# A split, modulated input kept in DRAM by the first of four passes and loaded by the other three

## The chip, the cores and the metric

One core of a Trainium2 chip. Its engines run side by side: PE (matrix products), DVE (vector), ACT (functions of one element, scaled copies), POOL, and SP, which here issues the DMAs. Each takes its instructions in the order that the build fixed, and waits at semaphores for the others. The metric is the device time of one execution in microseconds (us), lower is better.

## The reference

One layer for 4096 tokens of width 1024. `h = x * (1 + scale) + shift`, where shift, scale and gate come from a vector `c`; `proj = h @ w_in`, whose columns go to two kinds of heads; their outputs, normed and gated, are multiplied by `w_out`; then a layer norm.

```python
h = x * (1.0 + scale) + shift
proj = h @ w_in
# four heads of gated linear attention, in chunks of 64 tokens
S = d_n[..., None] * S + u_n                     # decay of the state, update
y_a = rms_norm(o_a, gla_norm_w) * silu(gla_og)
# four heads of the gated delta rule: convolution over 4 tokens, then per chunk
sol = triangular_solve(A + eye, rhs)             # unit lower triangular
v_new = u_n - w_n @ S
y_b = rms_norm(o_b, gdn_norm_w) * silu(gdn_og)
y = concatenate([y_a, y_b]) @ w_out
return layer_norm(ALPHA * x + (1.0 + gate) * y, ln_w, ln_b)
```

All of it is float32. The kernel takes operands of the large products in two parts of the type float32r: a head, which is the operand rounded, and a rest, which is what the head leaves. A product is three matmuls: head by head, head by rest, rest by head (`mm3`).

## The kernel before

The tokens are cut into 8 blocks of 512, the width into 8 k tiles of 128. Four passes go over all blocks, since the weights of one pass fill the room there is: two passes of gated linear attention with two heads each (GLA), then two of the delta rule with two heads each (GDN), then the output projection with the layer norm, block by block. What a pass makes of a block goes to DRAM (`y_spill`) until the end.

Every pass needs `h` of every block, in two parts. `prep_h` (L179 to L185) makes it anew each time: four loads `xt` of two k tiles each (512 KB), per k tile a modulation on DVE (L175), the head as a cast on ACT (L107), the rest as a subtraction on DVE (L64). The lines of `mod_split`:

```python
nc.vector.tensor_scalar(out=xt[:, j], in0=xt[:, j], scalar1=modc[:, 8 + k:9 + k],
                        scalar2=modc[:, k:k + 1], op0=mul, op1=add)
return split(xt[:, j], halves(hpool)(k))
```

`hpool` has 18 tiles of one part each: those of a block and one k tile more. `xpool` has three rooms of 512 KB; they serve `xt`, the raw weights of the next pass (`raw`) and some smaller things in turn.

The products of block n + 1 run while the recurrence and the norm of block n are worked off: `weave` lays a generator of small steps (`side`) into one of large products (`main`) and pins the order on PE by dependencies; where a small step stands among the products is written out by the numbers that the generators yield. The order on the other engines and on SP is a scheduler's. `h` of the next block is asked for right after a block's products.

In GLA a block's products are those for values (`pp<-wvl,h` in the first pass, `pp<-w,h` in the second), q, k and gate (`pp<-h,w`). Out of a low rank (`lr`, kept for the second pass in `lr_spill`) come the decays `e`, and from them W; the chunks' products are `pw<-VS,W`; `o` is scaled by its norm on DVE and transposed on PE (`pw<-ident,o`). The first block of all takes its products as the operands arrive (`first_block`).

In GDN a block has products for k, q, v and gate (all `pp<-h,w`), a convolution by three DVE steps each (`cacc`), the keys' sums of squares (`ssk`, on ACT by `jk`, then on DVE; `st` and `s` are the steps of its root), the products of keys (`AQ`) and the inverse of a triangular matrix. For the inverse the diagonal blocks of 32 go out (`u_spill`) and come back laid out for a solve on all partitions (`U`); the solve is a chain of 31 pairs of small DVE steps on `R`; `R` goes out (`r_spill`) and comes back as `Rd`, which DVE transposes to `Td` (L787). PE's products with `Td` and `Rd` put the inverse together, and the scan over chunks follows.

Of the kernel before, what the change touches and what calls it, by code (L numbers as in the profile page):

```python
# [13 lines left out]
F32 = mybir.dt.float32  # L14
F32R = mybir.dt.float32r
# [6 lines left out]
P = 128  # L22
D = 1024
KT = D // P  # 8 contraction tiles of the model width
TB = 512  # tokens of a block
# [6 lines left out]
def tile_hybrid(ctx, tc, xp, x, c, wada, bada, w_gla, w_vl, w_gdn, w_out, wup, bgate,  # L32
# [6 lines left out]

    ysp = nc.dram_tensor("y_spill", (NB, 4, P, 2, TB), F32).ap()  # L40
    lrsp = nc.dram_tensor("lr_spill", (NB, 80, TB), F32).ap()
# [6 lines left out]
    hpool = ctx.enter_context(tc.tile_pool(name="hpool", bufs=18))  # L48
# [3 lines left out]
    def share_banks(ph, n):  # L52
        """n of the 8 PSUM banks for the projections, the rest for everything else"""
        banks["proj"] = ph.enter_context(tc.tile_pool(name="pproj", bufs=n, space=PSUM))
        banks["work"] = ph.enter_context(tc.tile_pool(name="pwork", bufs=8 - n, space=PSUM))
# [15 lines left out]
    def keep_after(ins, other, reason):  # L71
        """the order of two instructions of an engine"""
# [4 lines left out]
    def in_order(ins):  # L77
        """functions that need a table keep their order on ScalarE, so that tables are loaded as
        seldom as the order has it"""
        if last_table[0] is not None:  # L80
            keep_after(ins, last_table[0], "table order")
        last_table[0] = ins
# [35 lines left out]
    # strict[c, j] = 1 where c > j  # L118
# [3 lines left out]
    # 1 + gate on every partition  # L122
# [11 lines left out]
    def mod_col(cb, wt, j, k):  # L134
        """column k of part j: 0 shift, 1 scale, 2 gate"""
# [27 lines left out]

    def halves(pool):
        return lambda k: [pool.tile([P, TB], F32R, name="h", tag="h") for _ in range(2)]
# [7 lines left out]
    def mod_split(xt, k):  # L173
# [3 lines left out]
        return split(xt[:, j], halves(hpool)(k))  # L177

    def prep_h(b):  # L179
        h = []  # L180
        for kk in range(4):
            xt = xpool.tile([P, 2, TB], F32, name="xt", tag="x")
            nc.sync.dma_start(out=xt, in_=xp[b, kk])
            h += [mod_split(xt, 2 * kk + j) for j in range(2)]
        return h  # L185

    def mm3(ps, lhs, rhs, first, last):
        """ps += lhs.T @ rhs, each (head, rest) of float32r: the three products that count."""
# [8 lines left out]
    def weave(side, main):  # L197
        """side's steps, each followed by as many of main's as it asks for; then the rest of main"""
# [13 lines left out]
    def rsqrt(pool, x, name):  # L212
        """x ** -0.5 of a small tile: a first guess from the exponent, and Newton's steps"""
# [13 lines left out]
    # a and b of the delta rule, by token  # L227
    abt = const.tile([P, NCH, 8], F32, name="abt")

    # ================= gate scalars of the delta rule =================  # L230
    # [token, head pair, (chunk, head of the pair)]
# [7 lines left out]
    def gate_scalars():  # L239
        tmp4 = xpool.tile([P, 8, P], F32, name="tmp4", tag="x")  # L240
        # mle[c, i] = 1 where c <= i
# [41 lines left out]
    # ================= gated linear attention, two heads a pass =================  # L283
    with ExitStack() as ph:
# [5 lines left out]
        # m64[64 * r + j, i] = 1 where j <= i  # L290
# [6 lines left out]
        # zero where a chunk of 64 starts  # L297
# [4 lines left out]
        # values of pass 0, and beside them the low rank gates and a and b: 256 + 16 + 8 columns  # L302
# [9 lines left out]
        # both parts of the gates' operands, one under the other: lr (head, head, rest), w (head, rest, head)  # L312
# [35 lines left out]
        def decays(t, lr):  # L348
            """exp of the sums of the log gates over a chunk of 64, in the four forms in use"""
# [26 lines left out]
        # W: left operand of [S' | o] = W.T [v ; S], rows (tokens, dk) of an even chunk,  # L376
        # (dk, tokens) of an odd one; columns (S', o) and (o, S')
# [17 lines left out]
        def from_k(kp, qt, W, e2, e4):  # L395
# [3 lines left out]
            # the two heads' operands lie in two halves of the array: a bank for each  # L399
# [19 lines left out]
        def values(t, b, wv, h, VS):  # L419
            """two token tiles at a time"""  # L420
# [32 lines left out]
        def finish(b, t, o, sg):  # L453
            """norm of o over a head, then its transpose times the norm's weight and the gate"""
# [20 lines left out]
        def weights():  # L475
            """v, q, k and gate of pass 1"""
# [6 lines left out]
        def first_block():  # L483
            """all products of a k tile as soon as its operands are there"""
            h, wt = [], {}
            ps = [proj_psum() for _ in range(3)] + [work_psum() for _ in range(8 - 3)]
            xt = None
            for k in range(KT):
# [16 lines left out]
                h.append(mod_split(xt, k))  # L505
# [23 lines left out]
        def block(t, b, h, W, VS, sg, first):  # L529
            """the block's products, and what follows each"""  # L530
            ahead = (t, b) == (1, NB - 1)  # weights of the next phase
# [30 lines left out]
        def before(st, VS):  # L562
            """chunks, norm and gate of the block before"""
# [9 lines left out]
        ws = []  # of the delta rule: columns of k, q, v, gate, two heads each  # L573
        for it in range(2 * NB + 1):
# [10 lines left out]
            if new:  # L585
# [5 lines left out]
                h = prep_h((it + 1) % NB)  # L591
# [5 lines left out]
    # ================= output projection and layer norm, by blocks =================  # L597
# [22 lines left out]
    def out_block(b, y, xres, lnw_sb, lnb_sb):  # L620
        for g in range(4):
# [6 lines left out]
            # the last tile of a block takes both halves at once, and so lets go of y as it goes  # L628
# [21 lines left out]
    # ================= gated delta rule, two heads a pass =================  # L650
    with ExitStack() as ph:
# [7 lines left out]
        # rows 0 to 63: the upper left inverses of 64; rows 64 to 127: products on the way  # L659
# [5 lines left out]
        def conv(t, b, i, ps):  # L665
            """causal convolution, i: 0 1 k, 2 3 q, 4 5 v; ps [128, 512]"""
# [14 lines left out]
        def decay_tiles(t, b, E):  # L681
            """E[j, (chunk, head), i] = exp(sum of g over j < c <= i), zero where j > i"""
# [20 lines left out]
        def sumsq(KQ, which, name):  # L703
            """sums of squares by token and RMS_EPS, and the transposes they were taken from"""
# [387 lines left out]
```

## Time and profile before

| | |
|---|---|
| median of 3 runs | 2206.84 us (2204.34 to 2214.05) |
| span of the profiled execution | 2214.4 us |
| PE busy | 2123.4 us (96%), 12868 matmuls |
| PE weight loads busy | 1789.0 us (81%), beside PE |
| DVE busy | 1593.8 us (72%) |
| ACT busy | 1078.2 us (49%) |
| DMA moved | 188.10 MB, mean 85 GB/s |

The page gives no time of the profiled execution beside its span; the span lies 0.3% above the median and as high as the slowest of the three runs. Busy time counts instructions at work, and matmuls overlap each other in their pipeline, so that a PE busy for 96% is not one at its peak. The clock in the rows is the share of full speed that PE was granted.

### The profile page before, as it was taken

What the parts mean: (1) busy time and instruction counts of PE and PEld (TensorE: products, weight loads), DVE (VectorE), ACT (ScalarE), POOL (GpSimd) and SP (SyncE); (2) the same over time, 40 slices, a digit from 0 to 9 for tenths busy, and PEclk for the clock granted to TensorE, in tenths of its full rate; (3) what the DMA queues carried; (4) which work ended last, traced back from release to release, by engine and by line L of the source; (5) the groups of instructions that cost most, each with busy time, mean ns of one, the idle gap of its engine ahead of it and who ended that gap; (6) DMA issues with size and microseconds to landing.
All of it is one profiled execution on the core that took longest, in us unless ns stands there. A gap on an engine that the chain in (4) does not pass through costs nothing.

```text
span 2214.4 us, 35705 instructions
## 1 busy us (share of the span) xinstructions
PE 2123.4 (96%) x12868; PEld 1789.0 (81%) x12868; DVE 1593.8 (72%) x4243; ACT 1078.2 (49%) x2685; POOL 205.4 (9%) x453
## 2 busy tenths in 40 slices
PE   6899999999999999999999999999999999999998
PEld 5788888878878778888888877888888777888886
DVE  7886776776577667867778677787677867766665
ACT  2655556645546545565554755556555462221110
POOL 1000000000000221011110121111111230000000
PEclk9999999999999989999999989999999999999999
DMA  7151123212113212121111321212112234353431
GB/s 279 65 164 51 54 89 98 74 66 87 52 51 128 79 34 64 52 65 46 37 63 63 103 72 34 64 52 65 48 36 62 61 93 148 143 198 135 140 107 76
DMA packets 89649, 188.10 MB, mean 85 GB/s; under 512 B 42704, under 2 KB 44800, under 8 KB 89472
## 3 DMA queue, kind: packets, MB, share of 16 engines
q1 hardware_dynamic: 89472, 185.82, 25.3%
q8 instruction: 101, 1.65, 0.3%
q14 instruction: 76, 0.62, 0.1%
HBM read 146.73 MB, written 39.06 MB: 84 GB/s over the span
## 4 chain that ended last, share of the span: by engine, by line
PE 66%; DVE 19%; ACT 4%; DMA 3%; issue 2%; SPq 0%; POOL 0%; DVEq 0%; ACTq 0%; POOLq 0%
PE pp L93 48%; PE pw L93 16%; PE pw L96 3%; DVE W L64 2%; DVE cacc L67 2%; DVE tp L64 2%; DVE R L64 2%; DVE e L64 1%; DMA xt<-xp 1%; DVE vp L64 1%; DVE xt L175 1%; ACT VS L107 1%; DVE o L64 1%; DVE h L64 1%; DVE bc L362 1%
## 5 line engine op out<-in xcount | busy, mean ns | idle before, releaser
L93 PE MATMUL pp<-h,w 128*128 128x512 f32 x4512 | 1147.3, 402 | 1.1 <-DVE W L64 1.1
L93 PEld LDWEIGHTS pp<-h,w 128*128 128x128 f32 x4512 | 828.3, 190 | 161.1 <-issue 1.7
L93 PE MATMUL pp<-w,h 128*128 128x512 f32 (+1 forms) x2112 | 421.1, 355 | 2.3 <-DVE w L64 1.1
L93 PEld LDWEIGHTS pp<-w,h 128*128 128x128 f32 x2112 | 349.4, 190 | 55.8 <-DVE w L64 1.7
L67 DVE SCALAR_TENSOR_TENSOR cacc<-u,convw_sb,cacc 128x512 f32<-128x512 f32 x288 | 220.7, 768 | 72.9 <-ACT cacc L99 70.1
L107 ACT CAST h<-xt 128x512 fp32r<-128x512 f32 x256 | 156.9, 619 | 133.4 <-PE pp L93 92.0
L64 DVE TENSOR_TENSOR h<-xt,h 128x512 fp32r<-128x512 f32 x256 | 175.1, 692 | 62.3 <-ACT h L107 38.4
L175 DVE TENSOR_SCALAR xt<-xt,modc 128x512 f32<-128x512 f32 x256 | 137.7, 554 | 28.3 <-DMA xt<-xp 27.8
L93 PE MATMUL pp<-wvl,h 128*128 128x280 f32 x744 | 117.1, 306 | 20.3 <-ACT h L107 19.1
L93 PEld LDWEIGHTS pp<-wvl,h 128*128 128x128 f32 x744 | 104.0, 196 | 23.6 <-ACT h L107 19.8
L99 ACT ACTIVATE rl<-mv,lnepscol 128x1 f32<-128x1 f32 x32 | 9.4, 295 | 225.3 <-DVE mv L641 211.3
L64 DVE TENSOR_TENSOR tp<-U,R 128x60 f32<-128x60 f32 (+24 forms) x496 | 115.4, 233 | 4.2
L64 DVE TENSOR_TENSOR R<-R,tp 128x60 f32<-128x60 f32 (+24 forms) x496 | 111.1, 224 | 4.6
L99 ACT ACTIVATE KQ<-cacc 128x512 f32<-128x512 f32 x64 | 40.5, 633 | 131.3 <-DVE cacc L67 131.1
L99 ACT ACTIVATE jk<-pw 128x128 f32<-128x128 f32 x256 | 71.8, 280 | 57.8 <-PE pw L96 52.6
L93 PE MATMUL pw<-VS,W 128*128 128x128 f32 x512 | 81.7, 283 | 4.1 <-DVE VS L443 2.8
L93 PE MATMUL pw<-S,KQ 128*128 128x128 f32 x512 | 85.0, 280 | 0.5 <-DVE S L67 0.5
L67 DVE SCALAR_TENSOR_TENSOR xres<-xres,pp 128x512 f32<-128x512 f32 x48 | 32.3, 682 | 71.9 <-PE pp L93 67.1
L107 ACT COPY u<-pp 128x512 f32<-128x512 f32 x96 | 56.4, 588 | 53.5 <-PE pp L93 45.9
L93 PEld LDWEIGHTS pw<-S,KQ 128*128 128x128 f32 x512 | 76.4, 195 | 6.3 <-DVE S L67 1.2
L107 ACT COPY o<-pw 64x256 f32<-64x256 f32 x128 | 46.8, 366 | 63.6 <-DVE VS L447 39.8
L99 ACT ACT_TABLE_LOAD x60 | 77.0, 1283 | 1.1
(328 smaller groups left out, 2926.3 us busy)
## 6 DMA issues: line engine op xcount, KB each, us to landing
xt<-xp SPq DMA_DIRECT2D x128, 512.0 KB
y_spill<-sg SPq DMA_DIRECT2D x32, 512.0 KB
yt<-y_spill SPq DMA_DIRECT2D x32, 512.0 KB
xres<-x SPq DMA_DIRECT2D x24, 512.0 KB
out_dram<-xres SPq DMA_DIRECT2D x24, 512.0 KB
mt<-wada SPq DMA_DIRECT2D x8, 1024.0 KB
raw<-w_gdn SPq DMA_DIRECT2D x16, 512.0 KB
U<-u_spill SPq DMA_DIRECT2D x64, 128.0 KB
```

The lines of the kernel that those rows point to most:

```text
L64: nc.vector.tensor_tensor(out=out, in0=a, in1=b, op=op)
L67: nc.vector.scalar_tensor_tensor(out=out, in0=a, scalar=s, in1=b, op0=op0, op1=op1)
L93: pe(nc.tensor.matmul(out, lhsT=lhsT, rhs=rhs, start=start, stop=stop))
L96: pe(nc.tensor.transpose(out, in_=in_, identity=identity))
L99: ins = nc.scalar.activation(out=out, in_=in_, func=func, **kw)
L107: nc.scalar.copy(out=out, in_=in_)
L175: nc.vector.tensor_scalar(out=xt[:, j], in0=xt[:, j], scalar1=modc[:, 8 + k:9 + k], scalar2=modc[:, k:k + 1], op0=mul, op1=add)
L362: nc.vector.tensor_tensor_scan(out=bc, data0=rmask, data1=mz, initial=0.0, op0=mul, op1=add)
```

## The change

In the first pass `make_h` does what `prep_h` did and then stores both parts of each k tile to a new DRAM tensor `h_spill` (`keep_h`: eight stores of 512 KB a block). In the other three passes `load_h` loads both parts of a k tile in one transfer of 512 KB, eight a block, straight into the operands, and there is no arithmetic on x. `hpool` now has 9 tiles of a pair each, the same room. The pools' other pairs follow (`halves`; `ypool` from 16 to 8). Comments are gone too.

```diff
+    hsp = nc.dram_tensor("h_spill", (NB, KT, P, 2, TB), F32).ap()
-    hpool = ctx.enter_context(tc.tile_pool(name="hpool", bufs=18))
+    hpool = ctx.enter_context(tc.tile_pool(name="hpool", bufs=9))
...
+    def pair(pool):
+        return pool.tile([P, 2, TB], F32R, name="h", tag="h")
...
-        return split(xt[:, j], halves(hpool)(k))
-
-    def prep_h(b):
-        h = []
+        t = pair(hpool)
+        return split(xt[:, j], (t[:, 0], t[:, 1])), t
+
+    def keep_h(b, tiles):
+
+        for k, t in enumerate(tiles):
+            nc.sync.dma_start(out=hsp[b, k], in_=t.bitcast(F32))
+
+    def make_h(b):
+        h, tiles = [], []
         for kk in range(4):
             xt = xpool.tile([P, 2, TB], F32, name="xt", tag="x")
             nc.sync.dma_start(out=xt, in_=xp[b, kk])
-            h += [mod_split(xt, 2 * kk + j) for j in range(2)]
+            for j in range(2):
+                parts, t = mod_split(xt, 2 * kk + j)
+                h.append(parts)
+                tiles.append(t)
+        keep_h(b, tiles)
         return h
 
+    def load_h(b):
+        h = []
+        for k in range(KT):
+            t = pair(hpool)
+            nc.sync.dma_start(out=t.bitcast(F32), in_=hsp[b, k])
+            h.append((t[:, 0], t[:, 1]))
+        return h
...
-                h.append(mod_split(xt, k))
+                parts, t = mod_split(xt, k)
+                h.append(parts)
+                tiles.append(t)
+            keep_h(0, tiles)
...
-                h = prep_h((it + 1) % NB)
+                h = make_h(it + 1) if it + 1 < NB else load_h((it + 1) % NB)
...
-                h = prep_h((it + 1) % NB)
+                h = load_h((it + 1) % NB)
```

The order of instructions moves in three places that matter below. The first is SP at the start, behind the last loads of the modulation's weights (`mt`): `xt` are block 1's loads, `lr_spill` is the store of block 0's low rank. Before:

```order
L490 DMA mt<-wada 128x2x1024
L183 DMA xt<-xp 128x1024 x6
L341 DMA lr_spill<-lr 80x512
L183 DMA xt<-xp 128x1024
L341 DMA lr_spill<-lr 80x512
```

Now:

```order
L516 DMA mt<-wada 128x2x1024
L191 DMA h_spill<-h 128x1024 x8
L197 DMA xt<-xp 128x1024
L367 DMA lr_spill<-lr 80x512
L197 DMA xt<-xp 128x1024 x2
L191 DMA h_spill<-h 128x1024
L197 DMA xt<-xp 128x1024
L191 DMA h_spill<-h 128x1024 x7
```

Block 0's eight stores stand ahead of block 1's first load, and the store of the low rank ahead of the second. The second place is PE at the same time: `pp<-wvl,h` here are block 1's first products, `pw<-e` those that need block 0's decays. Before:

```order
L93 MATMUL pw<-h,w 128x512 x12
L93 MATMUL pp<-wvl,h 128x280 x3
L96 MATMUL pw<-ident,lrt 80x128 x4
L93 MATMUL pp<-wvl,h 128x280 x6
L93 MATMUL pw<-lr,w_115 128x512
L93 MATMUL pp<-wvl,h 128x280 x63
L93 MATMUL pw<-e_515,e_513 64x64 x16
```

Now:

```order
L95 MATMUL pw<-h,w 128x512 x12
L98 MATMUL pw<-ident,lrt 80x128 x4
L95 MATMUL pw<-lr,w_115 128x512
L95 MATMUL pp<-wvl,h 128x280 x19
L95 MATMUL pw<-e_515,e_513 64x64 x16
```

Of block 1's products 72 stood ahead of `pw<-e`, now 19 do. The third place is DVE in the delta rule's second block, around the first `Td`; `cacc` are convolution steps, `ssk`, `st`, `s` the keys' sums of squares and their root. Before, the last steps ahead of it:

```order
L64 TENSOR_TENSOR s<-s,st 128x8
L67 SCALAR_TENSOR_TENSOR cacc<-u,convw_sb,cacc 128x512
L64 TENSOR_TENSOR st<-s 128x8
L64 TENSOR_TENSOR st<-st,ssk 128x8
L223 TENSOR_SCALAR st<-st 128x8
L787 STREAM_TRANSPOSE Td<-Rd 128x256
L64 TENSOR_TENSOR s<-s,st 128x8
```

Now:

```order
L66 TENSOR_TENSOR tp<-U,R 128x8
L69 SCALAR_TENSOR_TENSOR cacc<-u,convw_sb,cacc 128x512
L66 TENSOR_TENSOR R<-R,tp 128x8
L69 SCALAR_TENSOR_TENSOR cacc<-u,convw_sb,cacc 128x512 x5
L816 STREAM_TRANSPOSE Td<-Rd 128x256
L745 TENSOR_SCALAR ssk<-ssk 128x8
```

`Td` stood inside the root of the keys' sums of squares; now it stands ahead of the first step on them.

## Rows read from the trace of the kernel before

**Rows 1.** The page's busy times by engine, with shares of the span and instructions.

```profile
PE 2123.4 (96%) x12868; PEld 1789.0 (81%) x12868; DVE 1593.8 (72%) x4243; ACT 1078.2 (49%) x2685; POOL 205.4 (9%) x453
```

**Rows 2.** The page's granted clock in 40 slices, in tenths.

```profile
PEclk9999999999999989999999989999999999999999
```

**Rows 3.** The page's chain that ended last, by engine.

```profile
PE 66%; DVE 19%; ACT 4%; DMA 3%; issue 2%; SPq 0%; POOL 0%; DVEq 0%; ACTq 0%; POOLq 0%
```

**Rows 4.** Windows: length, busy us (instructions), granted clock, DMA share, GB/s.

```profile
1475.00:1540.00 65.00, 64.34 (x421) 54.02 (x421) 50.00 (x166) 36.44 (x98) 9.97 (x26) 1.00 0.18 55
...
813.60:834.20 20.60, 20.19 (x140) 0.52 0.00 1
834.20:857.00 22.80, 22.80 (x136) 1.00 0.40 120
1308.00:1321.70 13.70, 13.70 (x88) 0.50 0.23 78
1376.00:1383.00 7.00, 7.00 (x52) 0.52 0.01 2
1745.00:1752.00 7.00, 5.77 (x24) 0.52 0.25 75
```

**Rows 5.** PE's waits: for what, us in total, times, longest.

```profile
PE pw L96 <- DVE o L64: 21.2, 15, 2.4
PE pp L93 <- ACT h L107: 19.1, 3, 13.7
PE pw L93 <- DVE e L64: 7.2, 6, 4.0
...
PE pw L93 <- DVE Td L787: 3.2, 5, 0.9
```

**Rows 6.** The page's groups that make h: count, busy us, mean ns.

```profile
L107 ACT CAST h<-xt 128x512 fp32r<-128x512 f32 x256 | 156.9, 619 | 133.4 <-PE pp L93 92.0
L64 DVE TENSOR_TENSOR h<-xt,h 128x512 fp32r<-128x512 f32 x256 | 175.1, 692 | 62.3 <-ACT h L107 38.4
L175 DVE TENSOR_SCALAR xt<-xt,modc 128x512 f32<-128x512 f32 x256 | 137.7, 554 | 28.3 <-DMA xt<-xp 27.8
```

**Rows 7.** PE's timeline at three first Td products: start, us, [idle before].

```profile
814.01 1.02 PE L93 MATMUL pw<-Td,AQ 32*32 32x32 f32 x16 [4.01 <-DVE s L64]
...
1305.41 0.66 PE L93 MATMUL pw<-Td,AQ 32*32 32x32 f32 x16 [0.66 <-DVE Td L787]
...
1373.39 0.66 PE L93 MATMUL pw<-Td,AQ 32*32 32x32 f32 x16 [2.13 <-DVE st L64]
```

**Rows 8.** DVE's timeline ahead of the first of them.

```profile
803.29 0.17 DVE L64 TENSOR_TENSOR R<-R,tp 128x8 f32<-128x8 f32 x1
...
807.48 0.17 DVE L716 TENSOR_SCALAR ssk<-ssk 128x8 f32<-128x8 f32 x1 [2.93 <-ACT jk L99]
...
813.42 0.45 DVE L787 STREAM_TRANSPOSE Td<-Rd 128x256 f32<-128x256 f32 x1
```

**Rows 9.** SP's timeline there: the loads of Rd.

```profile
806.60 2.89 SPq L775 DMA_DIRECT2D Rd<-r_spill  x4
```

**Rows 10.** PE's timeline at the start.

```profile
64.12 8.26 PE L93 MATMUL pp<-wvl,h 128*128 128x280 f32 x63
76.39 1.13 PE L93 MATMUL pw<-e,e 64*64 64x64 f32 x32 [4.00 <-DVE e L64]
```

**Rows 11.** The chain of waits in the second GLA pass: start, us, what.

```profile
505.63 3.61 DMA xt<-xp
```

**Rows 12.** Window of the first 17.3 us, columns as in rows 4.

```profile
0.00:17.30 17.30, 3.20 (x12) 2.86 (x12) 7.57 (x12) 4.55 (x5) 3.78 (x17) 1.00 0.88 323
```

**Rows 13.** PE's timeline at a block's end in the second GLA pass.

```profile
536.92 8.44 PE L93 MATMUL pp<-h,w 128*128 128x512 f32 x36
...
544.74 2.88 PE L93 MATMUL pp<-h,w 128*128 128x512 f32 x12
...
553.26 1.68 PE L93 MATMUL pp<-w,h 128*128 128x256 f32 x12
```

More of the change, by code (lines that the diff above doesn't have):

```diff
@@ L162, in prep_w, with room @@
         return w
+    def pair(pool):
+        return pool.tile([P, 2, TB], F32R, name="h", tag="h")
     def halves(pool):
-        return lambda k: [pool.tile([P, TB], F32R, name="h", tag="h") for _ in range(2)]
+        def room(k):
+            t = pair(pool)
+            return t[:, 0], t[:, 1]
+        return room
     def split(src, room):
@@ L483, in first_block @@
         def first_block():
-            h, wt = [], {}
+            h, tiles, wt = [], [], {}
             ps = [proj_psum() for _ in range(3)] + [work_psum() for _ in range(8 - 3)]
@@ L1026, in tile_hybrid @@
         share_banks(ph, 3)
-        ypool = ph.enter_context(tc.tile_pool(name="ypool", bufs=16))
+        ypool = ph.enter_context(tc.tile_pool(name="ypool", bufs=8))
         fp = ph.enter_context(tc.tile_pool(name="fin", bufs=1))
```

## The prediction

> **What bounds the kernel now.** I read the busy times first [rows 1]: PE is busy 96% of the span, DVE 72%, ACT 49%. A change that takes work from DVE and ACT therefore pays only where PE stands still because of them, or where PE runs slowly afterwards. The page's clock row [rows 2] says that the granted clock is at its full level in most slices, with dips in two of them; the chain that ended last [rows 3] is 66% PE and 19% DVE. So there is a DVE share on the path, but most of DVE's 1594 us lies beside PE.
>
> The windows by stage [rows 4] say where. In a whole delta-rule block (1475 to 1540 us) PE is busy 64.34 of 65 us at clock 1.00: nothing is to be had there. In the 20.6 us after 813.6 the clock is 0.52, which is the lower of its two levels (1.2 GHz), in the 22.8 us after them 1.00 again; 13.7 us after 1308 are at 0.50, 7 us after 1376 at 0.52, 7 us after 1745 at 0.52. What runs at half speed costs half its time again. The waits of PE [rows 5] are small in sum: 21.2 us for DVE's `o` in 15 pieces, 19.1 us for ACT's `h` (three times, at the start), 7.2 us for DVE's `e`, 3.2 us in five pieces for `Td`.
>
> **What is removed.** In three passes of 8 blocks with 8 k tiles there are 192 modulations, casts and subtractions fewer, of 256 each [rows 6]. By their means that is 192 x (554 + 692) ns = 239 us of DVE and 192 x 619 ns = 119 us of ACT. In the delta rule (128 of the 192) PE is saturated, so I count this at nothing there: PE hides it, and if it did not, the windows would show PE idle. In the second pass of the gated attention (64) the one wait of each block is for `o`, 21.2 us / 15 = 1.4 us on the mean, at most 2.4. The work ahead of `o` on DVE is the decays, W and the root of the mean square, not x; its order is the same after the change. I keep this wait whole; bounds 0 and -21.2 us.
>
> **The one late transpose.** At 814.01 PE had stood for 4.01 us before the products of `Td` [rows 7]. The wait is put down to `s`, which is the instruction beside it; what PE needs is Td. DVE's row [rows 8] shows why Td is late: the solve of R ends at 803.29, `ssk` is taken up at 807.48 after an idle 2.93 us for ACT, and Td stands behind the whole root of `ssk`, at 813.42. R goes out to DRAM and comes back: the last of the four loads of Rd is issued by 806.60 + 2.89 = 809.5 us [rows 9], so Rd is there some 8 us after the end of R (an estimate: 6.2 to the last issue, and its way), at about 811. After the change two things move: 8 modulations and 8 subtractions no longer lie among the steps of R, so R ends up to 8 x 1.25 = 10 us earlier, and Td stands ahead of `ssk`. With R done only 5 us earlier, Rd is there at 806 and Td soon after, before PE asks at 814.01 - 4.01 = 810.0. So this wait goes: 4.01 us, and with it the slow stretch behind it, 20.6 us at 0.52, which is worth 20.6 x 0.48 = 9.9 us. The same at 1373: 2.1 us, put down to `st` [rows 7], and 7 us at 0.52, 3.4 us. The stretch after 1308 follows a wait of 0.66 us for Td and is 13.7 us at 0.50, 6.9 us; since PE idles as much in the block from 1475 to 1540 and its clock stays at 1.00 [rows 4], Td can't be all of its cause, and I take half, 3.4. Sum of gains: 4.0 + 9.9 + 2.1 + 3.4 + 3.4 = 22.8 us. Bounds: 0 (the Td waits stay) and 26.3 (the whole of 1308).
>
> The slow 7 us after 1745 (3.4 us lost) lie where the output weights are multiplied by the gate on POOL. Their raw loads now start much earlier, since the staging pool is no longer shared with x. Whether POOL's multiplication and DVE's part still fall there I can't read; 0 to -3.4, taken as 0.
>
> **The start.** Here the change costs something. PE's order shows that before the first `e` products there stood 72 products `pp<-wvl,h` of block 1, now 19. SP gets eight stores of block 0's h ahead of block 1's first x, and the store of the low rank gates, which waits for ACT, ahead of the second. In the trace 63 of these products took 8.26 us [rows 10], 131 ns each, and behind them PE still waited 4.00 us for `e`. The 53 products that move behind `e` no longer fill that gap: 53 x 0.131 = 6.9 us, unless `e` comes earlier because DVE no longer does block 1's modulation in between. Bounds 0 and 13 (the wait gets longer by 6.9, and the slow clock that now follows it lasts as much longer again). I take 6.9, the row's own price.
>
> **The stores and loads.** 64 stores and 192 loads of 512 KB come, 96 loads of x go: 64 MB more are read or written net of what goes. A 512 KB load takes 3.61 us from its issue to the DVE instruction that used it [rows 11]; the first 17.3 us of the program moved 323 GB/s [rows 12], at which 512 KB are 1.62 us. In a delta-rule block of 65 us that is 8 x 1.62 = 13 us of transfer, against a DMA share of 0.18 before.
>
> A load of tile k must wait until PE has used the old block's tile k - 1 for the last time (nine slots, one was free). In the second attention pass the gate products are the last, 48 matmuls from 536.92 on [rows 13], six to a tile. The first slot comes free at 536.92 + 6 x 0.227 = 538.3, its load is there at 541.9; with 1.62 us between loads the seventh is there at 551.6. Needed is it behind the first six of the twelve products at 553.26, at 554.1. Slack 2.5 us, so no wait: 0. It is thin: from 2.0 us a load on, PE waits.
>
> The Trainium skill (DMA: Bandwidth & Descriptors, section "Anatomy of one DMA") has a fixed cost of about 2 us on each transfer beside its bytes, and under "Bandwidth" advises transfers of 1 MiB or more. By it a 512 KB load alone would be some 3.2 us (an estimate from that page), and eight in a row that do not overlap would be the third rival below. The 3.61 us of the row agree with it for one load; the 323 GB/s of the other row say that loads issued together overlap.
>
> On SP the way of R out and back now stands behind these eight loads, and the loads wait for PE until the block's last products. In the order the last step of R still comes behind that point on DVE, so I cost this at 0. In the steady blocks Td now stands on DVE between two `vp` products (before, behind three convolution steps more); if Rd, 8 us behind R, were late there, `vp` and six convolution steps would wait, and with them the PSUM banks of the projections. Bounds 0 and the 4.01 us of the wait that I take away, in each of 16 blocks; I take 0, because the steps of R lose the modulations that lay among them.
>
> **Sum.** Gains 22.8, loss 6.9: -16 us. The profiled execution has a span of 2214.4 us, 7.6 us over the median of 2206.84; that is within the three runs (2204.34 to 2214.05), and nothing in the sum scales with it. Forecast 2206.84 - 16 = 2191 us.
>
> **Rivals.**
> 1. No change. The PE is the bound; the Td waits stay, or their place is taken by another wait in the same stretch (for Rd behind the loads on SP, or for `ssk`, whose chain still comes from ACT). Then only the start is felt: 2206.84 + 7 = 2214, or 2207 if `e` comes earlier. For it: 96% busy PE [rows 1]. Against it: Td's place in DVE's order, ahead of `ssk`.
> 2. More goes than I count: the `o` waits (21.2), the whole of 1308 (3.5 more), the slow stretch at 1745 (3.4). That gives 2191 - 28 = 2163. For it: DVE's copies of VS stand among x's modulations in the second attention pass. Against it: nothing of x is among the steps that lead to `o`.
> 3. Slower: loads do not overlap. One at a time, each 3.61 us: the seventh is there at 538.3 + 7 x 3.61 = 563.6, 9.5 us late, in each of the pass's eight blocks: 76 us, 2191 + 76 = 2267, and more if the delta rule's are late too. At 2.5 us a load it is 541.9 + 6 x 2.5 = 556.9, 2.8 us late: 22 us, 2213. It decides from 2.0 us on. For it: nothing in the old trace loads eight tiles in a row that each wait for PE. Against it: 323 GB/s with transfers of 512 KB and 1 MB in flight [rows 12].
> **How the numbers follow.** Forecast 0.52, first rival 0.24, second 0.10, third 0.14. About 0.5% (11 us) is what a measurement of this kernel can tell from no change: faster than 2196 or slower than 2218. The forecast's own range is 2178 to 2200 (bounds of the gains and of the start), of which I give nine tenths to faster: 0.47, with the second rival 0.57. The first rival, a tenth of the forecast and a part of the third are "same": 0.28. Slower has the rest, 0.15. The range of 8 in 10 goes from 2166, between the forecast and the second rival, to 2222, over the first rival's 2214 and the mild form of the third.
>
> **What would show it.** Right: no PE wait of 4 us before the first `Td` products and clock 1.00 behind them; DVE busy by about 240 us less, ACT by about 119; the steady delta-rule block still 67 us long. The start: a longer wait for `e` in the second block, and its products behind it. Wrong: PE waits for a DMA of `h` at the block boundaries (third rival); the Td wait still there, with r_spill issued late on SP (first); `o` waits gone (second).

## The result and the profile after

The changed kernel takes 2188.19 us (median of 4 runs, 2187.43 to 2193.93), the kernel before 2210.45 in the same runs (2204.34 to 2216.38). The ratio is 0.9897, with a 95% interval of 0.9876 to 0.9917: 1.0% faster. Forecast were 2191 us. The profiled execution of after has a span of 2186.3 us and a time of 2188.06, so 1.8 us lie around the span. With as much around it, that of before (2214.4) is 5.8 us above its median.

The page of after: busy times by engine, then the granted clock in 40 slices, then the chain that ended last by engine.

```profile
PE 2102.4 (96%) x12868; PEld 1772.8 (81%) x12868; DVE 1418.9 (65%) x3859; ACT 967.8 (44%) x2493; POOL 203.9 (9%) x453
...
PEclk9899999999999999999999999999999999999999
...
PE 79%; DVE 12%; ACT 4%; DMA 2%; issue 2%; POOL 0%; SPq 0%; DVEq 0%; POOLq 0%; ACTq 0%
```

Against [rows 1 to 3]: DVE has 175 us less, ACT 110, and PE's share stands as it was. DVE was expected to have 239 less; the durations of its instructions, added up, did fall by 239, but a page counts once what overlaps in them. The two dips of the clock in the middle are gone, one at the start is new. DVE's share of the chain fell from 19% to 12%.

PE's waits of after (us in total, times, longest):

```profile
PE pp L95 <- ACT h L109: 23.7, 5, 12.3
PE pw L98 <- DVE o L66: 20.9, 16, 2.3
PE pw L98 <- DVE vp L66: 7.8, 3, 5.9
...
PE pw L95 <- DVE e L66: 2.6, 4, 0.7
...
PE pw L95 <- DVE Td L816: 0.6, 1, 0.6
```

Against [rows 5]: the wait for `o` is untouched, that for `e` is small, the waits for ACT's `h` (the start) grew by 4.6 us, and there is a new one of 5.9 us for `vp`. No wait for a loaded `h` is in the list.

Windows of after (length, PE busy, granted clock, DMA share, GB/s): the stretch that was slow behind the first `Td`, a steady block, and the three longest slow stretches that after has.

```profile
813.60:834.20 20.60, 20.60 (x108) 1.00 0.27 75
...
62.00:76.00 14.00, 8.62 (x62) 0.52 0.64 223
1268.00:1274.00 6.00, 5.76 (x20) 0.50 0.02 10
1796.00:1803.00 7.00, 5.27 (x21) 0.53 0.23 75
1475.00:1540.00 65.00, 64.97 (x426) 1.00 0.28 87
```

The 20.6 us at 0.52 of [rows 4] run at 1.00. Over the whole span the mean clock went from 0.980 to 0.989: 2214.4 x 0.020 = 44 us given up before, 2186.3 x 0.011 = 24 after, so some 20 of the 28 us between these two spans are clock. The profiled execution of before was a poor one: over its 41 executions beside the runs below the clock goes from 0.977 to 0.989 and gives up 37 us on the mean, over the four of after (0.986 to 0.992) it is 24. By that some 13 of the 22 us between the medians are clock.

Where the time went can be read at points where the same products lie behind in both traces: after minus before, in us, with the times of before.

```
GLA pass 0, second block (92)                                     +2.7
GLA pass 1, last block (695)                                      +0.6
GDN, first block (779)                                            -1.7
behind the inverse at the first Td (843)                         -11.5
GDN, end of its first pass (1256)                                -12.0
ahead of the second pass's first Td (1290)                        -4.7
behind it (1333)                                                 -11.8
behind the Td after it (1392)                                    -16.8
ahead of the stretch at 1745 (1740)                              -18.5
behind it (1756)                                                 -25.5
ahead of the last blocks' waits (1819)                           -25.8
ahead of the last Td (1861)                                      -23.9
behind it (1896)                                                 -28.6
end of the last product (2205)                                   -28.1
```

The steps are worth 28 us where the medians differ by 22, since the profiled execution of before was slower than its median.

PE's own order moved at the Td products too, a fourth place beside the three named ahead of the prediction: 3361 large products (`pp`, and `pw<-h,w` of the first block) start ahead of the first Td product before, 3330 in after. So that product starting 10.9 us earlier is no gain of 10.9 us: 31 products of 0.227 us, 7.0 us of work, were put behind it.

The first `Td`, in DVE's timeline of after (start, us), and PE's products with it:

```profile
793.20 0.60 DVE L66 TENSOR_TENSOR R<-R,tp 128x8 f32<-128x8 f32 x1
...
802.52 0.45 DVE L816 STREAM_TRANSPOSE Td<-Rd 128x256 f32<-128x256 f32 x1
```

```profile
803.11 0.66 PE L95 MATMUL pw<-Td,AQ 32*32 32x32 f32 x16 [0.57 <-DVE Td L816]
```

R ends at 793.8, 9.7 us earlier than in [rows 8], where up to 10 was reckoned; the wait of 4.01 us [rows 7] is 0.57. PE asked for Td at 802.5, not at 810.0 as before.

The start, in PE's timeline and SP's:

```profile
63.45 4.57 PE L95 MATMUL pp<-wvl,h 128*128 128x280 f32 x18 [2.76 <-ACT h L109]
71.87 0.60 PE L95 MATMUL pp<-wvl,h 128*128 128x280 f32 x1 [3.85 <-ACT h L109]
72.54 1.14 PE L95 MATMUL pw<-e,e 64*64 64x64 f32 x32
```

```profile
39.17 15.30 SPq L191 DMA_DIRECT2D h_spill<-h  x8
54.52 0.42 SPq L197 DMA_DIRECT2D xt<-xp  x1
```

The eight stores hold SP for 15.3 us and block 1's loads come late, as reckoned; but `e` is ready at 72.54 where it was at 76.39 [rows 10], and that gives part of it back.

### The profile page after: what moved, and what is told of

It is laid out like the page before. It is cut to its first block, busy times and chain, and to the rows that moved or that the text cites. A ratio compares the mean times of both kernels' runs of the same rounds, so it can differ in the third digit from the quotient of the medians.

```text
span 2186.3 us, 35054 instructions
## 1 busy us (share of the span) xinstructions
PE 2102.4 (96%) x12868; PEld 1772.8 (81%) x12868; DVE 1418.9 (65%) x3859; ACT 967.8 (44%) x2493; POOL 203.9 (9%) x453
## 4 chain that ended last, share of the span: by engine, by line
PE 79%; DVE 12%; ACT 4%; DMA 2%; issue 2%; POOL 0%; SPq 0%; DVEq 0%; POOLq 0%; ACTq 0%
PE pp L95 58%; PE pw L95 17%; PE pw L98 4%; DVE W L66 2%; DVE e L66 1%; DVE o L66 1%; ACT VS L109 1%; ACT jk L101 1%; ACT la L101 1%; DVE tp L66 1%; DVE bc L388 1%; DMA xt<-xp 1%; DVE R L66 1%; DVE rst L66 1%; DMA mt<-wada 1%
## 5 line engine op out<-in xcount | busy, mean ns | idle before, releaser
L69 DVE SCALAR_TENSOR_TENSOR cacc<-u,convw_sb,cacc 128x512 f32<-128x512 f32 x288 | 232.7, 809 | 152.6 <-ACT cacc L101 105.7
L469 DVE COPY VS<-pw 64x256 f32<-64x256 f32 x64 | 26.7, 417 | 149.3 <-PE pw L95 149.0
L66 DVE TENSOR_TENSOR tp<-U,R 128x60 f32<-128x60 f32 (+24 forms) x496 | 109.0, 220 | 9.8
L66 DVE TENSOR_TENSOR R<-R,tp 128x60 f32<-128x60 f32 (+24 forms) x496 | 106.7, 215 | 10.9
L69 DVE SCALAR_TENSOR_TENSOR S<-S,edl,pw 128x128 f32<-128x128 f32 x128 | 42.3, 344 | 79.0 <-PE pw L95 77.7
L101 ACT ACTIVATE sg<-pp 128x512 f32<-128x512 f32 x62 | 36.4, 598 | 97.4 <-PE pp L95 95.2
L101 ACT ACTIVATE jk<-vp 128x128 f32<-128x128 f32 x128 | 39.9, 312 | 87.5 <-DVE vp L66 85.5
```

Of the source, the lines that this page charges most:

```text
L66: nc.vector.tensor_tensor(out=out, in0=a, in1=b, op=op)
L69: nc.vector.scalar_tensor_tensor(out=out, in0=a, scalar=s, in1=b, op0=op0, op1=op1)
L101: ins = nc.scalar.activation(out=out, in_=in_, func=func, **kw)
L469: nc.vector.tensor_copy(out=VS[0:64, g, 1, :], in_=pm[0:64, 0:256])
```

## The experiments

Twelve runs. Each median stands beside that of the kernel before on the same chip.

**1. Loads in the delta rule alone.** The second GLA pass makes h again:

```diff
-h = make_h(it + 1) if it + 1 < NB else load_h((it + 1) % NB)
+h = make_h(it + 1) if it + 1 < NB else (prep_h if it + 1 < 2 * NB else load_h)((it + 1) % NB)
```

Expected:

> The first pass stores h; only the two delta-rule passes load it, the second pass of gated attention makes h again. Theory (the gain is the delta rule's: the Td waits, the slow stretches behind them, and the change into the output projection): as fast as the full change, 2185 to 2192 us, no Td wait above 1 us before the second delta-rule block, clock 1.00 behind it. Rival (the gain needs the second attention pass without arithmetic on x, by its freed DVE and its free staging rooms): 2197 to 2206.

Measured: 2193.74 against 2210.57, ratio 0.9922 (0.9899 to 0.9944); its profiled span is 2187.3, the full change's 2186.3. By the same products it ends 27.1 us ahead of the kernel before, the full change 28.1. What the loads give comes from the delta rule's passes.

**2 and 3. Loads in the second GLA pass alone; no loads at all** (all passes make h, the first stores it):

```diff
+h = make_h(it + 1) if it + 1 < NB else (load_h if it + 1 < 2 * NB else prep_h)((it + 1) % NB)   # 2, prep_h in GDN
+h = make_h(it + 1) if it + 1 < NB else prep_h((it + 1) % NB)                                    # 3, prep_h in GDN
```

Expected:

> The first pass stores h; only the second pass of gated attention loads it, the delta rule makes h again. Theory: within 0.3% of the kernel before, 2203 to 2213 us, with the Td waits and the slow clock behind them as before; the wait for o in each block stays at 2.0 to 2.4 us. Rival: 2190 to 2197.

> The first pass makes and stores h as in the change, and all others make it again: the 64 stores alone, and the order at the start that comes with them. Theory: the start costs 1 to 3 us and the stores nothing else, 2207 to 2214 us. Rival (the stores or the order they force slow the whole first pass): the first pass longer by over 5 us, 2215 to 2225.

Measured: 2228.55 and 2232.26 against 2210.57, ratios 1.0102 (1.0065 to 1.0139) and 1.0101 (1.0069 to 1.0132). Both are about 1% slower. For run 2 no difference was expected: a miss. For run 3 the time is the rival's and above its range, but not by the rival's way, a longer first pass. The wait for `o` stays (22.3 us in 16 pieces in both), which is what was to be shown for the GLA pass. Directly ahead of the 16 first Td products PE stands 11.7 and 13.8 us in all; before it was 9.3, not only the 3.2 under Td's name in [rows 5], since the 4.0 under `s` and 2.1 under `st` are waits for Td as well.

Runs 1 and 3 differ in the delta rule's loads alone, and by 38.5 us. In run 1 PE stands 0.7 us ahead of the Td products in place of 13.8, and from 740 to 2100 us 17 us are at half the clock in place of 65: 13 and 24 us, nearly all of it. So within the new structure the arithmetic on x is worth more than the whole change, by these waits and the clock.

**4. The kernel before with Td pinned ahead of the keys' sums of squares:**

```diff
+    td_ins[0] = nc.vector.transpose(out=Td..., in_=Rd...)
...
+    ins = nc.vector.tensor_scalar_add(out=acc, in0=acc, scalar1=RMS_EPS)
+    if name == "ssk" and td_ins[0] is not None:
+        keep_after(ins, td_ins[0], "Td first")
```

Expected:

> The kernel before with one order pinned on DVE: in every delta-rule block Td stands ahead of the first step on the keys' sums of squares. All arithmetic on x is kept. Theory A (the place of Td in DVE's order made the wait of 4.0 us at 814): that wait falls to under 2 us, since Rd is there at about 811.5, and the slow stretch behind it goes or is halved; 2195 to 2204 us. Theory B (R's late end, for the modulations among its steps, made it): the wait stays at 2 us or more and the slow stretch with it, 2203 to 2212; ssk and with it the keys come later, too.

Measured: 2198.49 against 2210.57, ratio 0.9947 (0.9923 to 0.9972). DVE's timeline there, then PE's, then three windows (length, PE busy, clock, DMA share, GB/s):

```profile
802.34 0.17 DVE L64 TENSOR_TENSOR R<-R,tp 128x8 f32<-128x8 f32 x1
810.07 0.45 DVE L791 STREAM_TRANSPOSE Td<-Rd 128x256 f32<-128x256 f32 x1
```

```profile
810.66 0.66 PE L94 MATMUL pw<-Td,AQ 32*32 32x32 f32 x16 [1.63 <-DVE ssk L717]
```

```profile
812.00:826.00 14.00, 14.00 (x113) 0.52 0.01 1
1300.00:1325.00 25.00, 24.74 (x214) 1.00 0.36 107
1370.00:1390.00 20.00, 19.79 (x114) 1.00 0.39 112
```

One pinned order, without any arithmetic removed, gives about half of the change (12 us of 22), and PE's order is that of the kernel before. The wait falls from 4.01 to 1.63 us, but R still ends at 802.5, so Td is still late, and 14 us of slow clock follow. The slow stretches after 1308 and 1376 [rows 4] are gone. At the second the wait fell from 2.13 to 0.79 us; at the first it went only from 0.66 to 0.57, so that one trace can't show that the pin removed the stretch there. Theory A holds for the time and for most of the first wait, B for what is left of it.

**5. The full change with Td behind the whole root** (`inverse_head` called after `key_side`, and Td kept after the last step on `s`):

```diff
+    yield from key_side(new)
+    if last is not None:
+        inverse_head(last)      # Td kept after s
```

Expected:

> The full change, but with Td put behind the whole root of the keys' sums of squares on DVE in every delta-rule block (pinned). No arithmetic on x comes back. Theory A (the place of Td in the order is what costs): PE waits 2 to 5 us for Td in the second delta-rule block and at least as often as in the kernel before, with slow stretches behind the waits; 2195 to 2225 us. Theory B (what counts is that R ends early, since DVE has no arithmetic on x among its steps): at most 1 us of wait each, 2186 to 2193.

Measured: 2258.30 against 2207.37, ratio 1.0224 (1.0188 to 1.0260): 70 us off the full change, more than theory A said. A row of PE's waits and two windows:

```profile
PE pw L96 <- DVE Td L817: 25.2, 15, 4.3
```

```profile
812.00:826.00 14.00, 14.00 (x113) 0.51 0.01 1
1109.00:1123.00 14.00, 14.00 (x102) 0.51 0.12 39
```

15 waits of 1.7 us on the mean, with slow stretches of 10 to 20 us behind most of them; the mean clock of the four executions is 0.959 to 0.966. DVE has all of its freed time here, and it is not enough by itself. Two things moved together: with the call the copies out of Td and Rd on ACT and POOL went behind `key_side` too, and PE's order is another (3361 large products ahead of the first Td, as before, in place of 3330). How much of the 70 us is Td's place on DVE alone was not tried apart.

**6. The full change with the output weights' products on DVE** (POOL before):

```diff
-nc.gpsimd.tensor_tensor(out=raw3, in0=raw3, in1=colmul..., op=mul)
+nc.vector.tensor_tensor(out=raw3, in0=raw3, in1=colmul..., op=mul)
```

In after's timelines of POOL and of DVE stands why:

```profile
1256.47 4.75 POOL L156 TENSOR_TENSOR raw<-raw,grow 128x1024 f32<-128x1024 f32 x2
```

```profile
1256.49 2.45 DVE L66 TENSOR_TENSOR tp<-U,R 128x60 f32<-128x60 f32 x1
1258.87 2.38 DVE L249 TENSOR_SCALAR r_t<-r_t 128x8 f32<-128x8 f32 x1
```

Two DVE instructions of 0.2 us take 2.4 each while POOL multiplies; the staging rooms no longer shared with x let the first three of these weights come some 480 us earlier than before, into the change of pass.

Expected:

> The full change, with the eight products of the output weights and the gate on DVE in place of POOL. Theory (POOL's two products at 1256 to 1261 and one at 1264 hold up DVE's small steps, which take 2.4 us each there in place of 0.2, and make vp late, for which PE waits 5.9 us at 1268, with about 3.6 us lost at the low clock behind): the wait falls under 2 us and the slow stretch goes; 6 to 10 us faster than the full change, 2178 to 2183. Rival (vp is late for the order or the length of DVE's own work; DVE's products, 1.2 us each, then lie in the same place): 2186 to 2192.

Measured: 2179.44 against 2207.37, ratio 0.9869 (0.9835 to 0.9902). The time lies in the theory's range, but came another way. The wait for `vp` is 0.54 us, as it said. But by the same products the change of pass gives only 1 us against after: another wait, and a slow stretch behind it, took its place (PE's timeline, windows):

```profile
1288.55 0.66 PE L95 MATMUL pw<-Td,AQ 32*32 32x32 f32 x16 [1.27 <-DVE st L66]
```

```profile
1290.00:1300.00 10.00, 10.00 (x101) 0.51 0.01 2
1300.00:1310.00 10.00, 10.00 (x53) 0.80 0.08 13
```

Behind the first `Td` 4.6 us are lost, too: a slow stretch from 809 to 819, after waits of 0.9 and 0.4 us (0.6 and 0.8 in after, without one). The span is 6 us shorter for the other end of the delta rule: after's waits of 3.46 us for `zr` at 1798 and 1.53 for `vp` at 1821 are gone.

**7. The stores on POOL's queue:**

```diff
-nc.sync.dma_start(out=hsp[b, k], in_=t.bitcast(F32))
+nc.gpsimd.dma_start(out=hsp[b, k], in_=t.bitcast(F32))
```

Expected:

> The full change, with the 64 stores of h on POOL's queue in place of SP's, so that block 1's first loads of x and the store of the low rank no longer stand behind block 0's stores; PE's order at the start is that of the kernel before again (72 products ahead of the first e). Theory (the order on SP makes the waits of 2.8 and 3.9 us for ACT's h at 63 and 72): these waits go, the program is 1 to 4 us ahead of the full change from block 2 on: 2184 to 2188. Rival (the stores take the loads' time whatever queue they are on): no difference at block 2, 2187 to 2191, or slower if POOL's issue holds up its own work on the values' weights.

Measured: 2237.90 against 2207.37, ratio 1.0132 (1.0099 to 1.0165). Slower than either range: the whole loss lies in the first pass, some 41 us by block 7. The issues of DMAs (count, KB, median us to landing) and DVE's waits from 120 to 400 us:

```profile
h_spill<-h POOLq DMA_DIRECT2D x64, 512.0 KB, 7.1
```

```profile
DVE xt L183 <- DMA xt<-xp: 39.6, 18, 4.9
```

A store lands 7.1 us after its issue there (after's trace has no such time for SP's stores), and DVE waits 39.6 us for loads of x (6.8 in after, from 120 to 380 us). That the first causes the second was not tried.

**8. Every load of h in the second GLA pass doubled** (a second one, into rooms that nobody reads):

```diff
+sc = xpool.tile([P, 2, TB], F32, name="sc", tag="x")
+nc.sync.dma_start(out=sc, in_=hsp[b, k])
 t = pair(hpool)
 nc.sync.dma_start(out=t.bitcast(F32), in_=hsp[b, k])
```

Expected:

> The full change, with a second load of 512 KB, into spare staging rooms that nobody reads, ahead of each load of h in the second pass of gated attention. Forecast's reckoning (loads overlap; from about 2.0 us for each load of h PE waits at the end of a block): at 2 x 1.4 to 2 x 1.62 us for each the last one is some 3 to 8 us late in each of eight blocks, 2210 to 2250 us, PE waits for DMA of h. Rival (slack is larger than reckoned, or the loads overlap more): no waits, 2186 to 2192.

Measured: 2191.93 against 2207.37, ratio 0.9929 (0.9904 to 0.9955), span 2187.9. PE's waits for loaded h, SP's timeline (start, us), and a window (busy us of PE, PEld, DVE, ACT, POOL, then clock, DMA share, GB/s):

```profile
PE pp L95 <- DMA h<-h_spill: 1.4, 3, 0.6
```

```profile
508.71 17.59 SPq L210 DMA_DIRECT2D sc<-h_spill  x11
...
542.04 9.93 SPq L212 DMA_DIRECT2D h<-h_spill  x8
```

```profile
500.00:540.00 40.00, 37.74 (x261) 33.65 (x259) 17.04 (x45) 18.19 (x46) 0.00 (x0) 0.98 0.84 299
```

With a DMA share of 0.84 over 40 us PE waits 1.4 us in all. But the run does not test the reckoning: the second loads did not stay beside the loads of h. They were issued in rows of their own (`sc`), all of them by 526.3 us, and at the block's end SP issues eight loads of h in 9.93 us, as in after (9.86). The slack of 2.5 us, and the 2.0 us a load from which PE would wait, stay untested.

**9. The stores alone, with Td pinned first** (the edits of 3 and 4 together).

Expected:

> The run with the stores alone, where every pass makes h, and in addition Td pinned ahead of the keys' sums of squares on DVE. It asks why the stores alone were 1.0% slower than the kernel before. Theory A (the pairs of the new pool and the stores move DVE's order in the delta rule so that Td stands behind the root; PE waited 11.4 us for Td in 11 pieces): the Td waits fall under 4 us in all and the time to within 0.5% of the kernel before or below it, 2195 to 2212 us. Theory B (the stores or the coarser pool cost by themselves): 2220 to 2232.

Measured: 2218.10 against 2211.99, ratio 1.0028 (1.0010 to 1.0046), between the two theories' ranges. The pinned order takes back some 0.7 of the 1.0% of run 3, but not as theory A had it: PE still stands 12.1 us directly ahead of the first Td products (13.8 in run 3), 8.3 of it under Td's name in 9 pieces. What the pin gave it by, and what the coarser pool or the stores cost beside it, stays open.

**10. DVE work put back in the delta rule, Td pinned first:**

```diff
+sc = xpool.tile([P, 2, TB], F32, name="sc", tag="x")
+nc.vector.tensor_scalar(out=sc[:, 0], in0=t[:, 0]..., scalar1=modc..., scalar2=modc..., op0=mul, op1=add)
+tt(sc[:, 1], sc[:, 0], t[:, 1]..., sub)
```

Expected:

> The full change, with a modulation and a subtraction on DVE put back for every tile that the delta rule loads (on a tile that nobody reads, 256 DVE instructions of 0.55 and 0.69 us), and Td pinned ahead of the keys' sums of squares. Theory A (order, not DVE's freed time, is the gain): 2185 to 2197 us, Td waits under 4 us in all. Theory B (the freed time is at least half of it): 2198 to 2210, with the wait at about 803 back at 2 us or more.

Measured: 2229.85 against 2211.99, ratio 1.0081 (1.0056 to 1.0106), with 240 such instructions. It reads as theory B, and by more than B said, but it is no clean test. The work waits for loads, which wait for PE at the block's end (DVE's waits, then PE's):

```profile
DVE sc L213 <- DMA h<-h_spill: 17.0, 12, 2.0
```

```profile
PE pw L99 <- DVE vp L66: 17.5, 14, 7.3
```

In the kernel before x was there earlier. The work's tiles also come from the staging rooms that the change had freed, and PE waits 8.0 us once for a weight (`w`) at the change of pass. PE stands 3.1 us ahead of the first Td products, under theory A's 4, and the loss lies elsewhere. Inconclusive on size.

**11. Products on DVE, and Td pinned first** (6 and 4 together).

Expected:

> The full change with the output weights' products on DVE, and Td pinned ahead of the keys' sums of squares, for the wait of 1.3 us and the slow stretch of 14 us that the run with the products on DVE had at 1288. Theory (that wait is the place of Td again): no slow stretch there, 7 us off that run: 2168 to 2177 us. Rival (short waits ahead of the Td products stay whatever stands ahead of Td, and any of them can bring the slow clock): 2176 to 2183.

Measured: 2181.05 against 2211.99, ratio 0.9862 (0.9835 to 0.9890): no faster than 6. The rival holds, and more plainly than it was put. PE's timeline and windows:

```profile
1287.66 0.66 PE L96 MATMUL pw<-Td,AQ 32*32 32x32 f32 x16 [0.15 <-DVE ssk L746]
```

```profile
1290.00:1300.00 10.00, 10.00 (x102) 0.65 0.01 2
808.00:818.00 10.00, 10.00 (x61) 0.51 0.01 2
```

The wait is 0.15 us, PE is busy throughout, and the clock still falls. Between the small products of the inverse only 5, 2 and 4 large ones stand there (17, 16, 2 and 4 in after's steady block at 1208, which stays at 1.00). Run 10 has the same without any wait (PE's timeline, window):

```profile
1024.90 0.69 PE L96 MATMUL pw<-Td,AQ 32*32 32x32 f32 x16
...
1030.00:1040.00 10.00, 10.00 (x43) 0.50 0.01 2
```

**12. The wait for o.** To run 11, two steps of the gate's products ahead of the products with `e`, and the transposes of `o` later:

```diff
-            yield 6
+            yield 16
...
-            from_k(pk, qt, W, e2, e4)
+            if first is not None:
+                from_k(pk, qt, W, e2, e4)
...
                 for k in range(KT):
+                    if k == 2:
+                        from_k(pk, qt, W, e2, e4)
                     for hh in range(2):
                         proj_k(pg[hh], wg[hh], h, k)
```

Expected:

> The run with the products on DVE and Td pinned, and in addition two of the eight steps of the gate's products moved ahead of the products with e in each block of gated attention, with the transposes of o behind them: some 60 large products stand ahead of the first transpose of o in place of 50. It asks whether the wait for o (20.8 us in 16 pieces, which the full change left as it was) is a matter of PE's order. Theory: 10 products x 0.227 us = 2.3 us cover each wait of 2.3 us; the waits for o and e fall under 6 us in all, the slow stretches of 4 us behind every second one go (7 us), 2181 - 15 to 22 = 2159 to 2166 us. Rival (DVE's chain behind o gets later as PE's transposes do, so the wait comes back for e or for W): 2174 to 2182.

Measured: 2157.74 against 2208.97 (5 rounds), ratio 0.9755 (0.9735 to 0.9776): the fastest of all, 2.4% under the kernel before, and a little faster than the theory had it. Neither `o` nor a large wait for `e` is left in PE's list:

```profile
PE pp L96 <- ACT h L110: 26.4, 5, 13.6
PE pp L96 <- DVE abt L359: 4.9, 4, 1.9
PE pp L96 <- DVE W L66: 2.6, 3, 1.2
```

The slow stretches of 4 us in the GLA passes are gone with the waits. Two are left in the delta rule, 10 us at 0.50 behind the first Td and 14 us at 0.52 behind the last, after waits of 0.9 and 0.3 us.

## Why the prediction was right, step by step

The time fell within 3 us of the forecast, and the term that carried it, the Td waits with the slow clock behind them, had the right size in sum. Beside it, gains and losses that the sum did not have nearly cancel.

**The Td waits** (4.0 + 9.9 at 814, 2.1 + 3.4 at 1373, 3.4 at 1308; in all 22.8): by the same products 9.8 us from 779 to 843, 5.1 from 1333 to 1392, 7.1 from 1290 to 1333, in all 22.0. The sum is right; the first place gave 4 us less, and 1308 the whole of its 6.9 where half was taken.

The mechanism was half told. The forecast gave both, R's end 10 us earlier and Td ahead of `ssk`, and held that R only 5 us earlier would do, since PE asks at 810.0. In after PE asks at 802.5, because 31 large products that stood ahead of Td now stand behind it. So the whole 9.7 us of R were needed, and 0.57 us of wait are left. Run 4 shows that Td's place alone gives half of the change, run 5 that the freed time alone does not give it, and runs 1 and 3 what removing the arithmetic gives by the same waits. At 814 the place alone leaves 1.63 us and 14 slow us.

That no slow stretch stands behind the first Td in after is in part luck: of the seven traces with PE's order of after there and a wait of 0.5 to 0.9 us (after, runs 1, 6, 7, 8, 11, 12), three have 10 us at half the clock, 5 us lost.

**The cause of the slow clock** I put with the waits. Over the 14 traces there are 224 first Td products (16 blocks each). Where PE had stood 1.5 us or more directly ahead of one, a slow stretch began beside 18 of 19 (from 1.5 us ahead to 14 us behind it); with 1.0 to 1.5 us 8 of 16, with 0.15 to 1.0 us 11 of 46, with less 2 of 143. So the waits bear out, but they are not all of it. The two without a wait are run 10's, and run 11's 0.15 us is among the short ones; all three stand where the small products of the inverse have few large ones between them (4, 2 and 6; 5, 2 and 4; 5, 2 and 4). What decides there was not tried apart. At `o`, removing the wait removed the slow stretches (run 12).
The Trainium skill (TensorE: Matmul & The Clock Gate, section "HAM oscillation — how this bites in real kernels") puts such falls down to gaps in which PE is idle. The stretches behind `o` follow such gaps, of at most 2.4 us; those of runs 10 and 11 do not, with PE busy 10.00 of 10 us at 0.50 and 0.65.

**Taken as 0, or not in the sum, and wrong:** the passage from GLA to the delta rule gave -2.3 us between 695 and 779 (the wait of 2 us for VS and its slow stretch are gone). The stretch around 1745 gave -6.9 between 1740 and 1756. The prediction saw its slow clock and took it as 0; it did not see the wait ahead of it, for which POOL's products of the output weights held up DVE (before's POOL, DVE, PE):

```profile
1739.40 2.39 POOL L154 TENSOR_TENSOR raw<-raw,grow 128x1024 f32<-128x1024 f32 x1 [6.53 <-DVE S L67]
...
1739.70 2.14 DVE L64 TENSOR_TENSOR R<-R,tp 128x30 f32<-128x30 f32 x1
...
1746.23 1.22 PE L93 MATMUL pw<-zr,Rt 128*128 128x128 f32 x4 [3.25 <-DVE zr L67]
```

The other side of it was not seen: the same products, come forward, make a wait of 5.9 us at 1268 and cost 7.3 us with the slow clock behind it (1256 to 1290), and waits at 1798 and 1821 cost some 2 more. The last Td was in no term: before has 10 us at 0.51 behind it, after none, -4.6 us between 1861 and 1896, with waits of 0.21 and 0.05 us (a window of before):

```profile
1875.00:1885.00 10.00, 10.00 (x48) 0.51 0.11 34
```

The Trainium skill (SBUF — State Buffer, section "Who interferes with whom") says that a POOL instruction that reads SBUF and a DVE instruction with two inputs there, or one in a two-port mode, exclude each other for a whole instruction. The 2.45 and 2.38 us beside POOL's 4.75 for two agree.

**The start**, reckoned at +6.9: +2.7 at the second block, some +1.9 over most of the first pass and +0.6 at the end of the second. The row's price held for the products that moved, but `e` came 3.9 us earlier, the possibility that I named and did not take.

**The loads**, taken as 0: no wait for h. That loads do not overlap, the third rival, is off by after itself: eight of them are issued in 9.86 us, and from 540 to 552 us 305 GB/s are moved at a DMA share of 0.86. How thick the slack behind it is no run shows. The prediction's 3.2 us for one load rest on a section that is written for transfers issued by POOL; these are issued by SP. `o` was kept whole, and stayed: 21.2 before, 20.9 after.

**The range.** The forecast's own 2178 to 2200 does not follow from its bounds: with no gain and 13 us at the start they reach 2220.

Forecast were 22.8 - 6.9 = 16 us, measured 22 by the medians. That the two are close is luck as far as the terms go that the sum did not have.

## What to carry to other kernels

Where PE is busy all the time, work taken from other engines pays through what it does to PE's waits: look for the one small instruction that stands behind a long chain in a queue. Pinning it ahead gave half of this change without any arithmetic removed (run 4); in run 9 it did not make up for what the stores cost, and on top of run 6 it gave nothing (run 11), so it is to be tried and not assumed. A wait on a saturated PE can cost what the clock does afterwards as well: 9.9 us behind the 4.0 at 814, 6.9 behind the 0.66 at 1305, nothing behind most waits of that length. One execution says little about such stretches, since the same program gives up 24 to 51 us by them. Where a wait is left, large products that are ready can be moved in front of it: two steps of the gate's products in each block, in a few lines, took some 20 us off run 11 by the medians (24 by the ratios), about as much as the whole change.

## What the hardware showed that I had not expected

The granted clock can fall although PE is counted busy (run 11: 0.65 with 10.00 of 10 us busy behind a wait of 0.15 us; run 10: 0.50 with no wait at all). Two DVE instructions of 0.2 us took 2.4 each beside a POOL product of 2.4 us. Stores from POOL's queue took 7.1 us to land, and the first pass of that run was 41 us longer.
